# Two transformer blocks in one kernel: output parts that share a bank, copies tied to ScalarE, split remainders, gelu in stages, products ahead of the strips

## The chip, the core and the metric

The kernel runs on one core of a Trainium2 chip. The metric is device time in microseconds (us) of one execution. Five engines work beside each other, each through its own list of instructions in a fixed order: TensorE (PE, with PEld for its weight loads), VectorE (DVE), ScalarE (ACT), GpSimd (POOL) and SyncE (SP, which starts transfers). An engine stops at an instruction whose operands aren't ready, and everything behind it in its list stops too.

## The reference, cut to what matters

The input x has 512 tokens of 1024 float32 values and goes through two blocks.

```
block 1: p = rmsnorm(x) @ w_in            # q, k, v (8 heads of 64), u, vg (512 each), 8 forget gates
         att = softmax(q k^T/8 + cumsum(log sigmoid(forget)), causal) v
         u, vg = gelu(u), gelu(vg);  sg = u * (tril(w_spatial) @ rmsnorm(vg) + b)     # chunks of 128
         h = x + [att, sg] @ w_out;  h += conv_ffn(rmsnorm(h));  x = rmsnorm(h) * norm_final_g
block 2: mod = silu(c) @ w_ada + b        # six vectors: shift, scale, gate, twice
         p = modulate(rmsnorm(x)) @ w_in  # latents of q and kv, k_rope, cq, ck, cv
         o_ca  = chunk attention(rmsnorm(cq), rmsnorm(ck), cv, rel_bias)              # 8 heads of 64
         o_mla = latent attention: q, k from the latents, rmsnorm per head, rope      # 8 heads of 96
         x += g_a * ([o_mla, o_ca] @ w_out);  x += g_m * conv_ffn(modulate(rmsnorm(x)))
```

## The kernel before, in words

**Products.** Each float32 matrix product is three products of split operands: a weight is split into `whi` (a cast on ScalarE, L350) and a remainder `wlo` (raw minus `whi`, L351, on DVE, or on POOL where the plan says so), an activation into a pair of the same kind, and PE adds hi*hi, hi*lo and lo*hi in one of four PSUM banks with the tag `mm` (all through the helper at L372). `make_plan` (L279) lists the weight pieces in the order of use with a flag for POOL; pieces are loaded and split two ahead. Feature-major activations have one tile of 128 features by 512 tokens, x0 to x7.

**The order of PE.** It is the order in which the code issues. A `Fill` holds generators; `run(v)` lets them issue until about v ns of PE time are spent. `attention` (L619) walks over *strips*: a strip is one head's 128 queries against the 128, 256, 384 or 512 keys before their end. Block 1 has 32 strips, block 2 has 64: t0 to t31 of the chunk heads, t32 to t63 of the latent heads; t4, t8, t12 and so on are the narrow ones. A strip is: scores on PE (`s<-kh,qs` and `s<-kl,qs`), mask or bias and the row maximum on DVE (L597, a second small instruction reads the maximum out), exp on ScalarE (L601), transposes back on PE (`s<-ident,p`, L610), a copy `pt<-s` (L612), values on PE (`o<-vc,pt`). In PE's list the scores of strip t+2 stand before the transposes of strip t+1. Between these steps `fill.run` puts projections and output products whose inputs are there, and `bg.run` puts background jobs without PE work, or with little of it: norms, rope, and `final`, which scales x by block 1's last norm (x<-x,cols,mm, L942: two passes over x0 to x7, each pass from one bank).

**The order of the other engines.** A scheduler sorts their instructions by priority; background jobs get a lower one. The result is a fixed list per engine: where a list puts eight L942 instructions ahead of a strip's L597, that strip waits for them.

**The output product.** `gemm_part` (L403) multiplies one part of w_out with one pair of stacked attention tiles (`mix`), eight banks of 512 tokens each, and adds every bank to x on DVE (`x<-mm,x` L877 in block 1, `x<-mm,mod,x` L954 in block 2). It yields nothing until its own tiles are there. In block 2, `mix` tiles 0 to 3 come from the chunk heads in pairs, one tile every eight strips; part 0 needs the first two tiles, part 1 the other two. Parts 2 and 3 belong to the latent heads (`out_tail`).

**Norms of the latent heads.** `m_squares` (L1530) squares on POOL (`sqm<-mqk`, L1535), sums on DVE (`nw<-sqm`, L1536), a power on POOL (`nw<-nw,nhalf`, L526), a product on DVE (`mqk<-mqk,nw`, L1550), then the rope (`rt`, L1354 to L1357), and PE transposes (L1667). The chunk heads' norm does the same with `ca`, `sqc` and `ssc` (L1444 to L1457); PE transposes its result at L1633. The helper at L526 is the power of all norms.

**Gelu in block 1.** `gelu2` (L1108) takes one tile of 128x256: two steps on POOL, one on DVE (L1114), tanh on ScalarE, one on DVE (L1116), all issued at once. `qk(3)` evacuates a key projection at L1186 (`kf`), which PE waits for by way of its bank.

## Time and profile before

| | us |
|---|---|
| median of three runs (1226.94, 1228.15, 1228.16) | 1228.15 |
| the profiled execution | 1225.62 |
| its span | 1223.9 |
| PE busy | 1193.0 (97%) |
| DVE busy | 780.2 (64%) |
| ACT busy | 526.5 (43%) |
| POOL busy | 190.5 (16%) |

The profile is of one execution, 2.5 us under the median. From its start: projections of block 1 to about 70 us; attention 1 with its fill to about 215; the two feed-forward stages at 240 to 585 and at 866 to 1212; projections and norms of block 2 from 585; attention 2 from about 655 to 840; its output tail to 866. Busy time of PE is modelled: a matmul's row is longer than the distance to the next one (128x256: rows of 0.28 us that start every 0.115 us), so the idle time in rows of PE is what tells a wait. All times in what follows are us from the start of the span unless ns is said.

### The profile page before, as it was taken

The numbers are of one execution on the slowest core, as the hardware profiler recorded it, in microseconds if no ns is written. First come the engines' busy times: TensorE is split into PE (matmuls) and PEld (weight loads), VectorE is DVE, ScalarE is ACT, GpSimd is POOL, SyncE is SP. The second block draws the span as 40 slices with busy tenths as digits, with TensorE's granted clock in tenths as the row PEclk, the third lists the DMA queues.
The fourth block names the chain that finished last, engine by engine and source line by source line (L and its number), as shares of the span: only waits on it lengthen the run. The fifth ranks groups of instructions, "written<-read, shape, count | busy, mean of one in ns | idle before, by whom it ended". The sixth has DMA issues, their size and how long they took to land.

```text
span 1223.9 us, 17406 instructions
## 1 busy us (share of the span) xinstructions
PE 1193.0 (97%) x6730; PEld 1038.9 (85%) x6730; DVE 780.2 (64%) x1392; ACT 526.5 (43%) x946; POOL 190.5 (16%) x209
## 2 busy tenths in 40 slices
PE   9999898999999999999998989999999999999998
PEld 6898688988888888888998988899988888888887
DVE  6646777688888887433575878876675665653221
ACT  6535445454444443323434556655544444442110
POOL 2367301300000000000245472301200000000000
PEclk9999999999999999999999999999999999999999
DMA  7432222166666666433121333111133323233330
GB/s 237 120 102 78 82 82 61 53 188 196 200 192 190 193 190 190 144 98 128 58 86 57 87 109 104 36 36 36 53 123 102 103 86 104 93 89 112 114 110 18
DMA packets 42594, 135.78 MB, mean 111 GB/s; under 512 B 5120, under 2 KB 6016, under 8 KB 42512
## 3 DMA queue, kind: packets, MB, share of 16 engines
q1 hardware_dynamic: 34096, 106.84, 28.3%
q10 hardware_dynamic: 8208, 27.27, 7.4%
q8 instruction: 52, 0.85, 0.3%
q0 software_dynamic: 208, 0.57, 0.2%
q14 instruction: 30, 0.25, 0.1%
HBM read 128.37 MB, written 2.10 MB: 107 GB/s over the span
## 4 chain that ended last, share of the span: by engine, by line
PE 84%; DVE 6%; POOL 4%; issue 2%; ACT 2%; DMA 1%; SPq 0%; ACTq 0%; DVEq 0%; POOLq 0%
PE mm L372 74%; PE s L372 4%; PE o L372 3%; PE s L610 2%; POOL wlo L351 1%; ACT whi L350 1%; DVE wlo L351 1%; DVE s L597 1%; DVE ca L1457 1%; DMA x<-in_xT_dram 1%; POOL gelu L1111 0%; PE mm L1667 0%; DVE nt L557 0%; ACT p L601 0%; PE s L725 0%
## 5 line engine op out<-in xcount | busy, mean ns | idle before, releaser
L351 DVE TENSOR_TENSOR wlo<-wraw,whi 128x1024 fp32r<-128x1024 f32 (+4 forms) x182 | 210.3, 1157 | 180.6 <-ACT whi L350 179.5
L372 PE MATMUL mm<-xnh,whi 128*128 128x512 f32 (+1 forms) x832 | 310.8, 374 | 5.6 <-DVE x L877 2.7
L350 ACT CAST whi<-wraw 128x1024 fp32r<-128x1024 f32 (+4 forms) x194 | 191.6, 991 | 277.8 <-PE mm L372 260.2
L372 PE MATMUL mm<-xnl,whi 128*128 128x512 f32 (+1 forms) x832 | 309.7, 372 | 0.0
L372 PE MATMUL mm<-xnh,wlo 128*128 128x512 f32 (+1 forms) x832 | 309.7, 372 | 0.0
L372 PEld LDWEIGHTS mm<-xnh,whi 128*128 128x128 f32 x832 | 156.2, 188 | 33.5 <-DVE x L877 2.9
L372 PEld LDWEIGHTS mm<-xnh,wlo 128*128 128x128 f32 x832 | 156.1, 188 | 27.6
L372 PEld LDWEIGHTS mm<-xnl,whi 128*128 128x128 f32 x832 | 156.2, 188 | 26.7
L372 PE MATMUL mm<-gh,whi 128*128 128x512 f32 (+1 forms) x384 | 141.3, 368 | 1.1 <-DVE x L967 0.6
L372 PE MATMUL mm<-gh,wlo 128*128 128x512 f32 (+1 forms) x384 | 141.1, 367 | 0.0
L372 PE MATMUL mm<-gl,whi 128*128 128x512 f32 (+1 forms) x384 | 141.0, 367 | 0.0
L759 DVE SCALAR_TENSOR_TENSOR cv<-mm,cols,cv 128x510 f32<-128x510 f32 (+1 forms) x176 | 130.3, 745 | 2.5 <-ACT cv L757 0.5
L372 PE MATMUL mm<-whi,xnh 128*128 128x256 f32 (+3 forms) x304 | 96.5, 318 | 1.1 <-ACT xnh L842 1.1
L372 PE MATMUL mm<-wlo,xnh 128*128 128x256 f32 (+3 forms) x304 | 93.6, 308 | 0.2 <-DVE wlo L351 0.2
L372 PE MATMUL mm<-whi,xnl 128*128 128x256 f32 (+3 forms) x304 | 93.6, 308 | 0.1
L372 PEld LDWEIGHTS mm<-gh,whi 128*128 128x128 f32 x384 | 72.1, 188 | 13.5 <-DVE x L967 0.8
L372 PEld LDWEIGHTS mm<-gh,wlo 128*128 128x128 f32 x384 | 72.1, 188 | 12.1
L372 PEld LDWEIGHTS mm<-gl,whi 128*128 128x128 f32 x384 | 72.1, 188 | 12.0
L601 ACT ACTIVATE p<-s,st 128x128 f32<-128x128 f32 (+1 forms) x96 | 50.7, 528 | 70.4 <-DVE st L597 64.6
L1028 DVE CUSTOM_DVE_ANT_0 wada<-wada,cs,cols 128x1024 f32<-128x1024 f32 x48 | 61.5, 1282 | 28.9 <-DMA wada<-in_w_ada_dram 28.8
L372 PE MATMUL mm<-mix,whi 128*128 128x256 f32 (+1 forms) x288 | 73.8, 344 | 2.6 <-DVE x L877 1.5
L757 ACT ACTIVATE cv<-mm,cols 128x512 f32<-128x512 f32 x88 | 67.6, 773 | 0.0
(296 smaller groups left out, 1793.2 us busy)
## 6 DMA issues: line engine op xcount, KB each, us to landing
wraw<-in_w_up_dram SPq DMA_DIRECT2D x88, 512.0 KB, 3.6
wada<-in_w_ada_dram ACTq DMA_DIRECT2D x48, 512.0 KB, 3.7
wraw<-in_w_down_dram SPq DMA_DIRECT2D x32, 512.0 KB, 3.6
wraw<-in_w_out_dram SPq DMA_DIRECT2D x16, 512.0 KB, 3.7
wraw<-in_w_down_dram SPq DMA_DIRECT2D x16, 384.0 KB, 3.2
wraw<-in_w_qk_dram SPq DMA_DIRECT2D x8, 512.0 KB, 4.2
wraw<-in_w_v_dram SPq DMA_DIRECT2D x8, 256.0 KB, 4.9
x<-in_xT_dram SPq DMA_DIRECT2D x8, 256.0 KB, 6.5
```

The source lines that it names most:

```text
L350: nc.scalar.copy(hi[:, :n], raw[:, :n])
L351: (nc.gpsimd if pool else nc.vector).tensor_tensor(out=lo[:, :n], in0=raw[:, :n], in1=hi[:, :n].bitcast(F32), op=ALU.subtract)
L372: self.nc.tensor.matmul(out, lhsT, rhs, start=start, stop=stop, **kw)
L597: self.urgent = nc.vector.tensor_tensor_reduce(out=s[:, cs], in0=s[:, cs], in1=b, scale=1.0, scalar=3e38 if j == 0 else st[:, j - 1:j], op ...
L601: nc.scalar.activation(out=p[:, :nk], in_=s[:, :nk], func=AF.Exp, bias=st[:, len(parts) - 1:len(parts)], scale=-1.0, accum_out=hd["sums"](qi))
L610: self.nc.tensor.transpose(s[:, c], p[:, c], self.ident)
L757: nc.scalar.activation(out=t, in_=ps, func=AF.Identity, scale=w[2], bias=self.col(cb, n))
L759: nc.vector.scalar_tensor_tensor(out=t[:, d:], in0=ps[:, :512 - d], scalar=w[2 - d], in1=t[:, d:], op0=ALU.mult, op1=ALU.add)
L1028: nc.vector.tensor_tensor_reduce(out=w, in0=w, in1=self.cs, scale=1.0, scalar=self.col("b_ada_2", n), op0=ALU.mult, op1=ALU.add, accum_out ...
L1457: nc.vector.tensor_tensor(out=v3, in0=v3, op=ALU.mult, in1=ss[:, j, z, t].unsqueeze(2).to_broadcast([P, 4, 64]))
```

## The change

1. `gemm_first` replaces `gemm_part` for parts 0 and 1: both parts of an output tile add up in one bank (four matmul triples, then one addition to x). It yields nothing until the tiles of both parts are in `mix`. The plan lists these pieces in the order of use and flags parts 0 and 1 for POOL.
2. A remainder on POOL is made in steps of 256 columns.
3. Copies that `nc.any` spread over engines are ScalarE's: `pt`, `ca`, `kr`, `vc`, `mqk`, `vm`.
4. `gelu2` takes two tiles at once (128x512), yields between its stages, and its DVE steps have a late priority; the tiles have a pool of their own.
5. Block 1's fill has `turn(1)` right behind `spatial(1)`; block 2's fill has no `out1`; `final` moves from `cq0` to the second `mla`; the yield behind the rope tables is 3000, not 6000.
6. Ahead of attention 2, three rounds of `fill.run(1500)` and `bg.run(800)`; in it, the background rate is 1700 to strip 33, then 1200 (before: 1700 to strip 15, then 600).

```diff
         def parts(name, dest, skewed=()):
-            for p in range(4):
-                for g in range(2):
-                    plan.append((i[name][p, g], False, dest.get((p, g)), SKEW // 4 if p in skewed else 0))
+            for p, g in ((0, 0), (1, 0), (0, 1), (1, 1), (2, 0), (2, 1), (3, 0), (3, 1)):
+                plan.append((i[name][p, g], p < 2, dest.get((p, g)), SKEW // 4 if p in skewed else 0))
...
-            (nc.gpsimd if pool else nc.vector).tensor_tensor(
-                out=lo[:, :n], in0=raw[:, :n], in1=hi[:, :n].bitcast(F32), op=ALU.subtract)
+            step = 256 if pool else n
+            for o in range(0, n, step):
+                c = slice(o, min(o + step, n))
+                (nc.gpsimd if pool else nc.vector).tensor_tensor(
+                    out=lo[:, c], in0=raw[:, c], in1=hi[:, c].bitcast(F32), op=ALU.subtract)
...
+    def gemm_first(self, w, x, evac):
+        while not all(k in x for p in (0, 1) for k in PARTS[p]):
+            yield 0
+        cs = slice(0, 512)
+        for g in range(2):
+            hls = [self.weights([w[p, g]]) for p in (0, 1)]
+            for j in range(4):
+                ps = self.bank()
+                yield from self.part_tile(ps, [(hl[0], q, k) for p, hl in zip((0, 1), hls)
+                                               for q, k in enumerate(PARTS[p])], j, x, cs)
+                evac(4 * g + j, ps, cs)
...
-        self.nc.any.tensor_copy(out=pt[:, :nk], in_=s[:, :nk])
+        self.nc.scalar.copy(pt[:, :nk], s[:, :nk])
...
         def gelu2(v):
-            t = self.pp.tile([P, 512], F32, tag="p", name="gelu")[:, :256]
+            t = gl.tile([P, 2, 256], F32, tag="gl", name="gelu")
             nc.gpsimd.tensor_tensor(out=t, in0=v, in1=v, op=ALU.mult)
             nc.gpsimd.tensor_scalar(out=t, in0=t, scalar1=0.044715, scalar2=1.0, op0=ALU.mult,
                                     op1=ALU.add)
-            nc.vector.tensor_tensor(out=t, in0=t, in1=v, op=ALU.mult)
+            yield 800
+            with self.late():
+                nc.vector.tensor_tensor(out=t, in0=t, in1=v, op=ALU.mult)
...
             ("sp1", lambda: spatial(1)),
-            ("out0", lambda: self.gemm_part(i["w_out"], 0, mix, evac)),
             ("tu1", lambda: turn(1)),
-            ("out1", lambda: self.gemm_part(i["w_out"], 1, mix, evac)),
+            ("out0", lambda: self.gemm_first(i["w_out"], mix, evac)),
...
-            bg.add("final", final)
...
             if c == 0:
                 bg.add("kr", kr_rope())
+            else:
+                bg.add("final", final)
...
         def out0():
             bg.upto("final")
-            yield from self.gemm_part(i["w_out_2"], 0, mix, evac)
+            yield from self.gemm_first(i["w_out_2"], mix, evac)
...
-            ("out1", lambda: self.gemm_part(i["w_out_2"], 1, mix, evac)),
...
+        for _ in range(3):
+            fill.run(1500)
+            bg.run(800)
         self.attention(
             heads, fill,
             lambda t: 3000 if t < 0 else 2000 if t < 16 else 1600 if t < 34 else 500,
-            bg, lambda t: 1700 if t < 16 else 600, mix)
+            bg, lambda t: 1700 if t < 34 else 1200, mix)
```

What the change moves is seen in the engines' lists. First PE in block 2 at strips t21 to t23 before (`mm<-mix,w` are products of the output parts 0 and 1, `mm_7162` and so on their banks):

```order
L372 MATMUL mm_7150<-mix_6982,whi_7063 128x512 x2
L372 MATMUL mm_7150<-mix_6982,wlo_7064 128x512
L610 MATMUL s_7092<-ident_156,p_7097 128x128 x2
L372 MATMUL mm_7162<-mix_6587,whi_7063 128x512 x2
L372 MATMUL mm_7162<-mix_6587,wlo_7064 128x512
L372 MATMUL o_6985<-vc_5307,pt_7118 128x64
L372 MATMUL s_7167<-kh_6621,qs_6620 128x512
L372 MATMUL s_7167<-kl_6622,qs_6620 128x512
L372 MATMUL mm_7162<-mix_6982,whi_7063 128x512 x2
L372 MATMUL mm_7162<-mix_6982,wlo_7064 128x512
L610 MATMUL s_7133<-ident_156,p_7138 128x128 x3
L372 MATMUL mm_7191<-mix_6587,whi_7063 128x512 x2
```

In the list after, the same strips stand without them; `s_7116`, `s_7142` and `s_7162` are the scores of t21, t22 and t23 (and `s_7078` those of t20):

```order
L375 MATMUL s_7116<-kh_6650,qs_6649 128x256
L375 MATMUL s_7116<-kl_6651,qs_6649 128x256
L629 MATMUL s_7078<-ident_156,p_7083 128x128
L375 MATMUL o_7024<-vc_5271,pt_7111 128x64 x4
L375 MATMUL s_7142<-kh_6650,qs_6649 128x384
L375 MATMUL s_7142<-kl_6651,qs_6649 128x384
L629 MATMUL s_7116<-ident_156,p_7121 128x128 x2
L375 MATMUL o_7024<-vc_5271,pt_7136 128x64
L375 MATMUL s_7162<-kh_6650,qs_6649 128x512
L375 MATMUL s_7162<-kl_6651,qs_6649 128x512
L629 MATMUL s_7142<-ident_156,p_7147 128x128 x3
L375 MATMUL o_7024<-vc_5271,pt_7159 128x64 x2
```

From the scores of t20 to the transposes of t34 nothing but strips and some groups of four transposes of 128 columns stands in PE's list; the output products begin behind them.

DVE's list before, at strips t3 and t4 of block 2, has the first pass of `final` (`mm_6219` is its bank):

```order
L597 ISA s_6194,st_6197<-s_6194,bs_6026 128x512
L597 ISA st_6197 128x1
L942 SCALAR_TENSOR_TENSOR x0_83<-x0_83,cols_95,mm_6219 128x256
L687 TENSOR_TENSOR qs_6204<-mm_6210,qs_6204 64x512
L942 SCALAR_TENSOR_TENSOR x1_84<-x1_84,cols_95,mm_6219 128x256
L942 SCALAR_TENSOR_TENSOR x2_85<-x2_85,cols_95,mm_6219 128x256
L942 SCALAR_TENSOR_TENSOR x3_86<-x3_86,cols_95,mm_6219 128x256
L687 TENSOR_TENSOR qs_6207<-mm_6210,qs_6207 64x512
L351 TENSOR_TENSOR wlo_6254<-wraw_6251,whi_6253 128x256
L597 ISA s_6266,st_6269<-s_6266,bs_6108 128x128
```

After, that pass stands at t18 to t20 and the second at t21 and t22. DVE's list from t21 (`s_7116`) to t22 (`s_7142`) and the first of what follows:

```order
L616 ISA s_7116,st_7119<-s_7116,bs_6847 128x256
L616 ISA st_7119 128x1
L706 TENSOR_TENSOR qs_7039<-mm_7042,qs_7039 64x512
L716 SCALAR_TENSOR_TENSOR kl_7038<-mm_7085,gca_5258,kh_7037 64x512
L1666 TENSOR_SCALAR bs_7034<-bs_7034 128x512
L961 SCALAR_TENSOR_TENSOR x0_83<-x0_83,cols_95,mm_7054 128x256
L716 SCALAR_TENSOR_TENSOR kl_7041<-mm_7085,gca_5258,kh_7040 64x512
L616 ISA s_7142,st_7145<-s_7142,bs_6847 128x384
L616 ISA st_7145 128x1
L961 SCALAR_TENSOR_TENSOR x1_84<-x1_84,cols_95,mm_7054 128x256
```

Behind x7 of that pass come the sums, the scale and the products of the second latent group's norm, and only then the strip t23 (`s_7162`); the two small `st` rows between are the maxima:

```order
L961 SCALAR_TENSOR_TENSOR x7_90<-x7_90,cols_95,mm_7054 128x256
L1561 TENSOR_REDUCE nw_7067<-sqm_7098 128x4
L1561 TENSOR_REDUCE nw_7067<-sqm_7101 128x4
L1561 TENSOR_REDUCE nw_7067<-sqm_7104 128x4
L1568 TENSOR_SCALAR nw_7067<-nw_7067 128x16
L1575 TENSOR_TENSOR mqk_6856<-mqk_6856,nw_7067 128x768
L1575 TENSOR_TENSOR mqk_6857<-mqk_6857,nw_7067 128x768
L616 ISA s_7162,st_7165<-s_7162,bs_6847 128x512
L616 ISA st_7165 128x1
```

The second pass of `final` and the norm of `mqk_6856` and `mqk_6857` now both stand between the strips t22 and t23. The square sums in it come from POOL, whose list at that place has the output weights' remainders in steps, 16 instructions in four rows, ahead of the squares (`sqm`) and the power (`nw_7067`):

```order
L354 TENSOR_TENSOR wlo_6940<-wraw_6937,whi_6939 128x256 x4
L1667 MEMSET bs_6847 64x64
L354 TENSOR_TENSOR wlo_6990<-wraw_6987,whi_6989 128x256 x4
L354 TENSOR_TENSOR wlo_7439<-wraw_7436,whi_7438 128x256 x4
L354 TENSOR_TENSOR wlo_7448<-wraw_7445,whi_7447 128x256 x4
L1560 TENSOR_TENSOR sqm_7068<-mqk_6856 128x384
L1560 TENSOR_TENSOR sqm_7098<-mqk_6856 128x384
L1560 TENSOR_TENSOR sqm_7101<-mqk_6857 128x384
L1560 TENSOR_TENSOR sqm_7104<-mqk_6857 128x384
L1667 MEMSET bs_7034 64x64
L545 TENSOR_TENSOR nw_7067<-nw_7067,nhalf_161 128x16
```

In the list before, these remainders were on DVE (`wlo_7107`, `wlo_7147` and the like, one instruction of 1024 columns each).

## Rows read from the trace of the kernel before

**Rows 1.** The page, busy time of each engine and share of the span.

```profile
PE 1193.0 (97%) x6730; PEld 1038.9 (85%) x6730; DVE 780.2 (64%) x1392; ACT 526.5 (43%) x946; POOL 190.5 (16%) x209
```

**Rows 2.** Windows: length; engines' busy us (instructions); PE clock; DMA share; GB/s.

```profile
640.00:660.00 20.00, 16.59 (x135) 15.99 (x134) 13.56 (x17) 7.70 (x12) 15.04 (x9) 0.98 0.25 86
702.00:726.00 24.00, 20.00 (x168) 19.39 (x167) 17.57 (x45) 11.36 (x30) 17.14 (x23) 1.00 0.37 94
763.00:772.00 9.00, 8.29 (x61) 7.12 (x61) 8.09 (x23) 5.86 (x17) 3.58 (x6) 1.00 0.19 61
```

**Rows 3.** Waits of PE: total us, times, longest us.

```profile
PE mm L1633 <- DVE ca L1457: 3.4, 2, 2.2
PE mm L372 <- DVE kf L1186: 2.3, 1, 2.3
```

**Rows 4.** Timeline of DVE, block 1: start, us, instruction, idle before and releaser.

```profile
127.20 0.42 DVE L1114 TENSOR_TENSOR gelu<-gelu,uv 128x256 f32<-128x256 f32 x1 [1.22 <-POOL gelu L1112]
127.54 0.68 DVE L1186 TENSOR_TENSOR kf<-mm,rrow 128x512 f32<-128x512 f32 x1
```

**Rows 5.** Timeline of PE, block 1.

```profile
128.28 0.50 PE L372 MATMUL mm<-xnh,whi 128*128 128x512 f32 x1 [2.29 <-DVE kf L1186]
...
148.86 0.70 PE L372 MATMUL mm<-uv,wsp 128*128 128x256 f32 x2 [2.59 <-DVE mix L745]
```

**Rows 6.** Timeline of POOL at the start of attention 2.

```profile
652.95 2.67 POOL L351 TENSOR_TENSOR wlo<-wraw,whi 128x1024 fp32r<-128x1024 f32 x1
655.77 2.34 POOL L351 TENSOR_TENSOR wlo<-wraw,whi 128x1024 fp32r<-128x1024 f32 x1 [0.16 <-ACT whi L350]
```

**Rows 7.** Timeline of DVE, block 2, from there to strip t16.

```profile
652.91 5.81 DVE L1457 TENSOR_TENSOR ca<-ca,ssc 128x256 f32<-128x256 f32 x4 [3.01 <-POOL ssc L526]
...
682.20 2.83 DVE L942 SCALAR_TENSOR_TENSOR x<-x,cols,mm 128x256 f32<-128x256 f32 x7
...
702.59 0.70 DVE L597 CUSTOM_DVE_ANT_0 s<-s,bs 128x512 f32<-128x512 f32 x1 [1.17 <-PE s L372]
...
703.81 2.01 DVE L1457 TENSOR_TENSOR ca<-ca,ssc 128x256 f32<-128x256 f32 x4
...
712.16 0.76 DVE L697 SCALAR_TENSOR_TENSOR kl<-mm,gca,kh 64x512 fp32r<-64x512 f32 x1
...
717.08 0.96 DVE L1550 TENSOR_TENSOR mqk<-mqk,nw 128x768 f32<-128x768 f32 x1 [3.02 <-POOL nw L526]
...
725.64 0.28 DVE L597 CUSTOM_DVE_ANT_0 s<-s,bs 128x128 f32<-128x128 f32 x1
```

**Rows 8.** Windows of 3 us at the start of attention 2, as rows 2.

```profile
658.00:661.00 3.00, 2.55 (x14) 2.36 (x15) 2.17 (x5) 1.10 (x2) 0.11 (x1) 0.72 0.17 49
661.00:664.00 3.00, 3.00 (x21) 3.00 (x21) 2.12 (x3) 2.13 (x4) 0.00 (x0) 0.71 0.29 64
```

**Rows 9.** Chain of waits, block 2: start, us, engine and line.

```profile
665.26 2.07 PE mm L372 x18
...
679.40 0.44 PE s L610 x4
...
684.13 0.84 PE o L372 x8
```

**Rows 10.** Groups by line and shape: xcount, busy us, mean ns, idle before.

```profile
L942 DVE SCALAR_TENSOR_TENSOR x<-x,cols,mm 128x256 f32<-128x256 f32 x16 | 6.8, 473 | 0.2
...
L351 POOL TENSOR_TENSOR wlo<-wraw,whi 128x1024 fp32r<-128x1024 f32 x12 | 29.3, 2443 | 6.8 <-ACT whi L350 6.7
...
L601 ACT ACTIVATE p<-s,st 128x512 f32<-128x512 f32 x24 | 16.5, 688 | 14.2 <-DVE st L597 11.6 <-PE mm L372 2.4
...
L1535 POOL TENSOR_TENSOR sqm<-mqk 128x384 f32<-128x384 f32 x8 | 7.5, 932 | 12.8 <-ACT p L601 5.3 <-PE s L610 3.8 <-DVE nw L1536 3.5
...
L687 DVE TENSOR_TENSOR qs<-mm,qs 64x512 fp32r<-64x512 f32 x8 | 5.5, 688 | 1.1 <-ACT qs L686 0.9
...
L1536 DVE TENSOR_REDUCE nw<-sqm 128x4 f32<-128x384 f32 x8 | 4.4, 545 | 0.1
```

## What the rows say of the change: the prediction

> **What bounds the kernel now.** I read the page's busy times first: PE is busy 97% of the span, DVE 64%, ACT 43%, POOL 16% [rows 1]. The number of PE's instructions stays as it was, so the change can only win from the time in which PE waits, or add to it. Next come the windows of both attention stages. Of the 20 us before strip t0 of block 2, PE is busy 16.6; of the 24 us around strips t11 to t16, it is busy 20.0, while POOL works 17.1 and DVE 17.6; in 763 to 772, where PE's list already holds bare strips before, it is still busy 8.3 of 9 [rows 2]. The list of PE's waits then names who ends them: `kf` at L1186 and `ca` at L1457, both by DVE [rows 3]. The timelines show what stood ahead of them: `kf` is behind a gelu step that itself waited 1.22 us for POOL [rows 4], and PE's product waits 2.29 us for that [rows 5]; at 652.91, four `ca` instructions take 5.81 us [rows 7].
>
> **Step A, block 1.** The gelu steps go late in DVE's list, behind `kf`: of the 2.29 us, all goes; the wait of 2.59 us for `mix` (L745) at 148.86 [rows 5] stays, since `turn(1)` stands right behind `spatial(1)` and has no output product between. The additions to x become 8 instead of 16; at one or two of them PE waits for the bank, and I put 0.7 us on that. The copies that go to ScalarE and the four remainder tiles per block that go from DVE to POOL lie beside PE's work: cost nothing, gain nothing, unless POOL is late for a weight. Four tiles at 2.44 us on POOL [rows 10] are 9.8 us, and one late tile holds PE for at most those 2.4 us. A = -3, between -6 (the spatial wait goes too) and +1.
>
> **Step B, ahead of strip t0 of block 2.** PE waits 3.4 us in all for `ca` [rows 3], and behind the wait the granted clock is 0.72 and 0.71 of full for two windows of 3 us [rows 8]: 6 x 0.285 = 1.7 us more. The change puts 42 products of 256 columns there. 18 such take 2.07 us [rows 9], 0.115 each, so 42 take 4.8 us: longer than the wait. These 4.8 us are not new, they are taken from later strips. B = -4.8, between -5.5 and -2 (the next wait in the chain, for `qs`, then shows).
>
> Why the four `ca` took 5.81 us is seen beside them: POOL ran two remainders of 1024 columns from 652.95 to 658.1 [rows 6], and the same four instructions at 703.81 took 2.01 us [rows 7]. The Trainium skill has a rule for it ("SBUF — State Buffer", section "Who interferes with whom"): a VectorE instruction with two SBUF inputs and a GpSimd one that reads SBUF keep each other out for the whole instruction. The trace agrees, 5.81 against 2.01 us. By this rule steps of a quarter hold such an instruction for 0.6 us at a time, not 2.4: at most 4 x 0.6 on top of 2.01, 4.4 us instead of 5.81. B would stay what it is, since the products cover either.
>
> **Step C, strips t8 to t18.** From the DVE instruction of strip t11 (702.59) to that of t16 (725.64) are 23.05 us [rows 7], in a window where PE is idle 4.0 us [rows 2]: DVE and a power on POOL (3.02 us of waiting on it) set the pace. After, DVE has in these strips no copies of `pt`, `vm` or `mqk` and fewer remainders, and the PE time with it is unchanged. C = -4, between -5.5 (everything idle in t8 to t18) and -1 (ScalarE, which has the copies, is then late for the exp: 0.69 us each [rows 10]).
>
> **Step D, strips t18 to t34.** Here the change takes work from PE and gives work to DVE. Part 0 of the output product began at t21 before; `gemm_first` waits for all four tiles of the chunk heads, the last of which is ready after t31. In PE's list from t18's scores to t23's transposes are then 12 products of 256 columns (1.4 us), six pairs of scores (17 times 256 columns, 2.0 us), 25 transposes (0.11 each by the row of four in 0.44 us [rows 9]: 2.8 us), 26 value products at 0.105 [rows 9] (2.7 us) and four products with `ms`, taken as eight of 0.11 (0.9 us): 10 us. In DVE's list between the same points stand, by rows of the same forms:
> - both passes of `final`, 16 at 2.83/7 = 0.40 us [rows 7]: 6.5
> - five strips' mask and maximum, 0.28 to 0.70 [rows 7]: 2.7
> - one `mix` and two `qs` at 0.69 [rows 10], two `kl` at 0.76 [rows 7], one `bs`: 4.0
> - four sums at 0.55 [rows 10] and a scale: 2.4
> - the wait for the power, 3.02, and two `mqk` at 0.96 [rows 7]: 4.9
>
> That is 20.5 us, and the exp of t23 on ScalarE (0.69 [rows 10]) with its sum read out adds 0.9. Rows of DVE overlap by some 0.07 us (0.47 is the mean row of L942 [rows 10], 0.40 its share in the run of seven), so I take 1.2 off for the 17 others: 20 us against 10. PE runs out of what it can do at the transposes of t22 and t23 and waits 10 us. Two things come on top. POOL's list has four remainder tiles (9.8 us) and four squares (0.93 each [rows 10]) ahead of that power, and the last tile is cast on ScalarE in t18; DVE's first sum stands ahead of the last two x of the first pass, so I take 3 us of waiting for it. Behind t23 come ten more strips without fill; in 763 to 772 four to five such strips lose 0.7 us [rows 2], so ten lose 1.5 to 2. D = 10 + 3 + 2 = +15. Ends: +7, where POOL is in time, scores run ahead of DVE at t18 and the bare strips pass as fast as before; +20, where the POOL wait doubles and ScalarE, which has four copies of `vm`, a cast of 1024 columns and the first `qs` between the exps of t18 and t19, adds its own.
>
> PE's clock is weighed here too. After the wait at 658 it was 0.72 and 0.71 [rows 8], and in D PE waits longer. The Trainium skill's page "TensorE: Matmul & The Clock Gate" (section "HAM oscillation — how this bites in real kernels") says that idle gaps send the array back to half its clock, and that each gap pays anew. The rows agree for one gap: 1.7 us. By the rule D would be 16 to 18, but PE has idle time to lose in that stretch, so in the sum it has nothing.
>
> **The sum.** -3 - 4.8 - 4 + 15 = +3.2 us. The profiled execution took 1225.62 us, so one after would take 1228.8. The median of the runs is 1228.15, 2.53 us above it: forecast 1231.4. The bound of what can be told from no change is 0.2%, 2.45 us, so it is slower beyond 1230.6.
>
> **Rivals.**
> 1. *The gap in the fill is shorter than its list, and the kernel gets faster.* The mechanism is slack: the scores of two strips stand ahead of each transpose, DVE idles in t14 to t18, where PE has fill, and each strip's exp needs only its own strip. If D costs +6, the sum is -3 - 4.8 - 4 + 6 = -5.8, or 1222.3. It decides at D under 9.3 us. For it: the bare strips at 763 to 772 lost little with 8.1 of 9 us of DVE busy [rows 2]. Against it: DVE's list is fixed, both passes of `final` and the norm stand ahead of t23, and none of those 20 us of work can be passed by.
> 2. *Gains and loss cancel.* With D between 9.4 and 14.2 the sum lies within 2.4 us either way; also if A, B and C give half (-6) and D is its 7 (+1). Time 1228.
> 3. *POOL becomes the bound.* The steps of remainders and DVE's two-input instructions hold each other, so that squares, power and a weight come late together. The four `ca` lost 3.8 us to two tiles [rows 6, 7]; block 2 has four tiles more on POOL, 7.6 us at that rate. Then D = 20 and C = 0: -3 - 4.8 + 20 = +12, or 1240. For it: POOL was busy 17.1 of 24 us at t11 to t16 already [rows 2]. Against it: a step holds for a quarter of the time.
>
> **How the numbers follow.** The forecast's case (D from 14.3 to 19, 1230.6 to 1236) has 0.34, the faster one 0.31, the cancelling one 0.21, POOL as the bound 0.14. Slower: 0.34 + 0.14 = 0.48; the same: 0.21; faster: 0.31. The range runs from 1220 (A, B and C as taken, D = 4) to 1241 (the third rival); the forecast's own is 1230 to 1236. What is left out on either side is about one in ten.
>
> **What would show it.** In the profile after, strips t19 to t24 of block 2 take over 15 us, PE waits 2 to 5 us at t22's transposes and 5 to 9 at those of t23, both ended by ScalarE's exp and behind it by DVE; POOL's squares start right behind the remainders, and the strip's L597 of t23 starts right behind the two `mqk`. `kf` no longer ends a wait, no wait for `ca` over 1 us stands ahead of t0, and the clock holds 1.00 there. The forecast is wrong if PE's waits in t18 to t34 come to under 9 us, or if a new wait, for a weight's remainder or for the exp, shows over 3 us elsewhere.

## The result, and the profile after

The changed kernel takes 1243.86 us (median of runs from 1239.95 to 1249.09) beside 1227.55 for the kernel before on the same chip: 1.0139 times as long, interval 1.009 to 1.0187. That is slower, as forecast, but by 16.3 us, where the forecast's sum had +3.2, and the median lies above the range's end of 1241 (two of the four executions, 1239.95 and 1240.48, lie just under it). The profiled execution took 1247.23 us (span 1245.0), 21.6 more than that of before.

The page after, busy times; it answers to [rows 1]:

```profile
PE 1205.5 (97%) x6730; PEld 1050.2 (84%) x6730; DVE 747.0 (60%) x1312; ACT 535.3 (43%) x974; POOL 216.3 (17%) x257
```

DVE has 33 us less and POOL 26 more; PE has the same 6730 instructions and 12.5 us more of them. So PE was not only made to wait: of the 21.1 us by which the span grew, 8.6 are waiting (39.5 us without work against 30.9), and 12.5 are PE running slower.

Windows show both. A row's loss is its length less PE's busy time, plus busy time times (1 - granted clock). The first fence holds windows of the kernel before that [rows 2] don't have (block 1; strips t1 to t10 and t17 to t29 of block 2; the stretch where the last norm begins), with the columns as there:

```profile
80.00:240.00 160.00, 147.12 (x923) 128.75 (x922) 109.72 (x262) 73.15 (x167) 52.40 (x58) 1.00 0.26 76
660.00:702.00 42.00, 41.50 (x329) 40.85 (x328) 30.33 (x73) 22.02 (x53) 13.94 (x14) 0.97 0.28 76
726.00:763.00 37.00, 36.94 (x254) 33.77 (x253) 31.31 (x68) 25.60 (x61) 13.26 (x14) 1.00 0.38 114
763.00:790.00 27.00, 26.03 (x187) 23.29 (x188) 22.62 (x60) 16.78 (x47) 12.13 (x15) 1.00 0.13 40
845.00:890.00 45.00, 44.10 (x340) 42.28 (x339) 30.31 (x56) 26.40 (x50) 10.68 (x14) 1.00 0.16 50
```

The same windows, and the two of [rows 2], after:

```profile
80.00:240.00 160.00, 150.90 (x921) 132.34 (x920) 96.67 (x229) 74.00 (x165) 64.90 (x74) 0.97 0.26 76
640.00:660.00 20.00, 20.00 (x171) 20.00 (x170) 10.13 (x13) 7.87 (x15) 16.38 (x15) 1.00 0.25 81
660.00:702.00 42.00, 39.62 (x311) 38.98 (x310) 23.41 (x54) 25.45 (x65) 18.40 (x25) 0.96 0.29 79
702.00:726.00 24.00, 22.56 (x177) 21.66 (x176) 17.44 (x44) 12.06 (x34) 17.23 (x22) 1.00 0.40 115
726.00:763.00 37.00, 22.16 (x136) 20.45 (x135) 22.59 (x59) 17.13 (x46) 26.19 (x38) 0.67 0.28 87
763.00:790.00 27.00, 26.48 (x185) 23.70 (x185) 15.95 (x46) 17.65 (x50) 6.72 (x7) 0.95 0.00 1
845.00:890.00 45.00, 42.20 (x326) 40.89 (x325) 29.87 (x60) 19.34 (x40) 10.17 (x13) 0.96 0.21 71
```

| Stretch | loss before | loss after | difference | forecast |
|---|---|---|---|---|
| 80 to 240 (A) | 12.9 idle + 0 clock | 9.1 + 4.5 | +0.7 | -3 |
| 640 to 702 (B) | 3.9 + 1.6 | 2.4 + 1.6 | -1.5 | -4.8 |
| 702 to 726 (C) | 4.0 | 1.4 | -2.6 | -4 |
| 726 to 790 (D) | 1.0 | 15.4 + 7.4 | +22 | +15 |
| 845 to 890 | 0.9 | 2.8 + 1.7 | +3.6 | none |

The clock of a window is a mean that counts its idle time too, so D's 7.4 is summed from windows of 4 us. The differences add up to +22, where the two profiled executions differ by 21.6. The clock column has two digits, so a row can be off by half a us, and the agreement is no closer than that.

The waits of PE after (total, times, longest); `ca` and `kf` of [rows 3] have no row any more:

```profile
PE s L629 <- ACT p L620: 18.1, 9, 7.4
PE mm L375 <- ACT sq L515: 2.5, 1, 2.5
...
PE s L375 <- DMA kh<-kh: 1.4, 1, 1.4
...
PE mm L375 <- DVE mix L764: 1.1, 1, 1.1
PE s L375 <- DMA kl<-kl: 1.0, 1, 1.0
```

Three waits for an exponential make up 14.84 us of D. PE's timeline there (the scores of t18, then x4, x2 and x4, the transposes of t19, t21 and t23):

```profile
729.65 0.42 PE L375 MATMUL s<-kh,qs 128*128 128x384 f32 x1
...
738.25 0.89 PE L629 MATMUL s<-ident,p 128*128 128x128 f32 x4 [2.48 <-ACT p L620]
...
750.78 0.69 PE L629 MATMUL s<-ident,p 128*128 128x128 f32 x2 [7.36 <-ACT p L620]
...
759.74 1.11 PE L629 MATMUL s<-ident,p 128*128 128x128 f32 x4 [5.00 <-ACT p L620]
```

The chain of waits through that stretch (start, us, engine and line) has nothing of PE from 735.79 to 759.74:

```profile
735.81 4.84 POOL wlo L354 x7
740.65 0.79 POOL sqm L1560
...
746.92 2.74 DVE x L961 x7
749.66 1.39 DVE nw L1561 x3
...
751.33 2.91 POOL nw L545
754.27 0.97 DVE mqk L1575
...
755.30 1.10 POOL rt L1381
...
758.41 0.47 POOL mqk L1386
758.90 0.34 ACT p L620
...
759.74 1.11 PE s L629 x4
```

In words: remainders of weights on POOL, then the squares of the second latent group, `final`'s second pass, the sums, the power, the products, the rope. These are two pieces of background (the norm of the second `mqk`, `final`) and the remainders, all within 23 us. And the exponentials wait for more than their masks. The next three fences show POOL's remainders there, the masks of t18, t21 and t23 on DVE, and the exponentials of t21 and t23 on ScalarE:

```profile
729.51 2.83 POOL L354 TENSOR_TENSOR wlo<-wraw,whi 128x256 fp32r<-128x256 f32 x4
...
732.38 8.28 POOL L354 TENSOR_TENSOR wlo<-wraw,whi 128x256 fp32r<-128x256 f32 x12
```

```profile
730.49 0.56 DVE L616 CUSTOM_DVE_ANT_0 s<-s,bs 128x384 f32<-128x384 f32 x1
...
742.72 0.43 DVE L616 CUSTOM_DVE_ANT_0 s<-s,bs 128x256 f32<-128x256 f32 x1
...
756.01 0.69 DVE L616 CUSTOM_DVE_ANT_0 s<-s,bs 128x512 f32<-128x512 f32 x1
```

```profile
750.16 0.47 ACT L620 ACTIVATE p<-s,st 128x256 f32<-128x256 f32 x1 [4.74 <-DVE nw L1561]
...
758.90 0.69 ACT L620 ACTIVATE p<-s,st 128x512 f32<-128x512 f32 x1 [4.88 <-POOL mqk L1386]
```

t18's and t23's masks bound the stretch that D reckoned with; t21's is done at 743.2, its exponential starts 7 us later and waits for `nw`, a sum of squares: its tile comes from the pool `pp2`, three tiles shared with the squares (`sqm`) and the rope's products.

### The profile page after: what moved, and what is told of

Read it like the earlier page. It is cut to its first block, busy times and chain, and to the rows that moved or that the text cites. A ratio compares the mean times of both kernels' runs of the same rounds, so it can differ in the third digit from the quotient of the medians.

```text
span 1245.0 us, 17431 instructions
## 1 busy us (share of the span) xinstructions
PE 1205.5 (97%) x6730; PEld 1050.2 (84%) x6730; DVE 747.0 (60%) x1312; ACT 535.3 (43%) x974; POOL 216.3 (17%) x257
## 4 chain that ended last, share of the span: by engine, by line
PE 87%; DVE 4%; POOL 4%; ACT 2%; issue 2%; DMA 1%; SPq 0%; ACTq 0%; DVEq 0%; POOLq 0%
PE mm L375 77%; PE s L375 4%; PE o L375 3%; PE s L629 2%; POOL wlo L354 1%; DVE s L616 1%; DMA x<-in_xT_dram 1%; DVE nt L576 1%; PE mm L1693 0%; DMA cs<-in_c_dram 0%; POOL nw L545 0%; ACT p L620 0%; PE s L744 0%; ACT whi L349 0%; PE r L375 0%
## 5 line engine op out<-in xcount | busy, mean ns | idle before, releaser
L354 DVE TENSOR_TENSOR wlo<-wraw,whi 128x1024 fp32r<-128x1024 f32 (+5 forms) x174 | 200.5, 1155 | 182.9 <-ACT whi L349 181.9
L1047 DVE CUSTOM_DVE_ANT_0 wada<-wada,cs,cols 128x1024 f32<-128x1024 f32 x48 | 61.5, 1282 | 30.8 <-DMA wada<-in_w_ada_dram 30.8
L545 POOL TENSOR_TENSOR rstd<-rstd,nhalf 128x2 f32<-128x2 f32 x6 | 5.1, 858 | 363.9 <-DVE rstd L554 363.9
```

What stands on the lines that cost most here:

```text
L354: (nc.gpsimd if pool else nc.vector).tensor_tensor(out=lo[:, c], in0=raw[:, c], in1=hi[:, c].bitcast(F32), op=ALU.subtract)
L545: self.nc.gpsimd.tensor_tensor(out=x, in0=x, in1=e, op=ALU.pow)
L1047: nc.vector.tensor_tensor_reduce(out=w, in0=w, in1=self.cs, scale=1.0, scalar=self.col("b_ada_2", n), op0=ALU.mult, op1=ALU.add, accum_out ...
```

## Experiments

Each time stands beside that of the kernel before on the same chip (1227.6 to 1228.1 us). The last columns are read from each profile: PE's longest wait for an exponential in the whole kernel (in e8, e13 and e18 it lies in block 1), and PE's busy time and clock in the 37 us from 726. PE's waits for other things are not in the column: e1 has one of 5.9 us for `mix`, e2 one of 5.6 for a bank that `final` reads, e4 one of 6.6 for `att`, e14 and e15 one of 3.7 and 3.4 ahead of a score.

| Run | Edit to the changed kernel | us | ratio to before, interval | wait | busy, clock |
|---|---|---|---|---|---|
| after | - | 1243.86 | 1.0139, 1.009 to 1.0187 | 7.4 | 22.2, .67 |
| e1 | `final` early | 1239.73 | 1.0097, 1.0082 to 1.0112 | 5.6 | 24.7, .71 |
| e2 | parts apart | 1237.71 | 1.0081, 1.0054 to 1.0108 | 4.7 | 24.1, .82 |
| e3 | remainders on DVE | 1239.61 | 1.0101, 1.0084 to 1.0118 | 6.1 | 23.0, .68 |
| e6 | e3 + e1 | 1236.33 | 1.0068, 1.0053 to 1.0083 | 7.9 | 24.7, .72 |
| e7 | e6 + e2 | 1226.21 | 0.9995, 0.9979 to 1.0012 | 5.2 | 30.8, .91 |
| e4 | squares' own tiles | 1249.44 | 1.0173, 1.0158 to 1.0188 | 5.2 | 26.2, .77 |
| e10 | four tiles | 1240.96 | 1.011, 1.0082 to 1.0137 | 6.0 | 22.9, .63 |
| e12 | e7 + e10 | 1225.91 | 0.9986, 0.9972 to 0.9999 | 4.0 | 30.8, .95 |
| e5 | scores repeated | 1243.07 | 1.0124, 1.0107 to 1.0141 | 3.6 | 28.6, .77 |
| e11 | rate of before | 1228.86 | 1.0006, 0.999 to 1.0022 | 6.2 | 29.2, .86 |
| e14 | e11 + e1 | 1229.23 | 1.0016, 1.0002 to 1.003 | 1.7 | 30.2, .86 |
| e15 | e14 + e10 | 1230.56 | 1.0016, 1.0001 to 1.0031 | 2.0 | 29.5, .91 |
| e16 | before + new rate | 1235.76 | 1.0063, 1.0045 to 1.0081 | 1.3 | 31.9, 1.00 |
| e8 | e7 + rate, rope, copies | 1220.58 | 0.9938, 0.9918 to 0.9957 | 0.9 | 34.5, 1.00 |
| e13 | e8 + e10 | 1215.28 | 0.9897, 0.9868 to 0.9926 | 0.9 | 35.2, 1.00 |
| e17 | e13, joined, POOL | 1226.59 | 0.9996, 0.9978 to 1.0014 | 5.2 | 29.4, .86 |
| e18 | e13, joined | 1219.17 | 0.9923, 0.9907 to 0.994 | 0.9 | 32.8, 1.00 |
| e19 | e13, POOL | 1219.64 | 0.9932, 0.9914 to 0.9949 | 1.0 | 34.8, 1.00 |

**One part undone at a time (e1, e2, e3), and together (e6, e7).**

```diff
 e1:  bg.add("rope", rope())
+     bg.add("final", final)          # and no longer behind the second mla
 e2: -yield from self.gemm_first(i["w_out_2"], mix, evac)
     +yield from self.gemm_part(i["w_out_2"], 0, mix, evac)
     +("out1", lambda: self.gemm_part(i["w_out_2"], 1, mix, evac)),   # and the plan's order
 e3: -plan.append((i[name][p, g], p < 2, ...
     +plan.append((i[name][p, g], p < 2 and name == "w_out", ...
```

> The kernel after, with the job `final` back in `cq0` (its 16 instructions on DVE then stand at strips t0 to t3). Theory 1 (DVE's list: both passes of `final` ahead of the masks of t18 to t23 make the wait): PE's waits for the exp in t18 to t24 fall from 14.8 us (2.5 + 7.4 + 5.0) to 5 to 8, the clock recovers sooner, time 1231 to 1236. Rival (POOL's chain: the remainders ahead of the squares, and the exp behind both): the waits stay over 11 us, time 1240 or more.

> The kernel after, with parts 0 and 1 of block 2's output product one after the other again (part 0 may start with the first two tiles, plan in that order; their remainders stay on POOL in quarters). Theory 1 (the gap in the fill is the root, DVE's and POOL's lateness only shows because of it): waits for the exp in t18 to t34 under 4 us, clock 1.00 there, time 1221 to 1227. Rival (DVE and POOL are late by themselves): waits over 8 us stay, time over 1234.

> The kernel after, with block 2's four remainder tiles of parts 0 and 1 back on DVE, whole (four instructions, 4 x 1.23 = 4.9 us more on DVE, 11.1 us of steps less on POOL). Theory 4 (the two runs before have shown that neither the place of `final` nor the gap in the fill is enough: POOL is late, its remainders stand ahead of the squares, and tiles, banks and exps wait behind them): PE's waits in t18 to t24 fall from 14.8 us to 5 to 9, time 1231 to 1237. Rival, theory 1 (DVE's list is what is too long): DVE has more to do, the waits stay over 13 us, time 1242 or more.

> The kernel after with two edits: block 2's remainders on DVE, whole, and `final` in `cq0`. Theory 4 with theory 1 as its second half: POOL's lateness and the 6.5 us of `final` each cover the other, and with both gone the waits in t18 to t34 fall under 5 us, time 1226 to 1232. Rival, theory 5 (a stretch of 15 strips without fill costs by itself, since each strip's chain is longer than PE's part of it): over 8 us of waits stay, time 1236 or more.

> The kernel after with three edits: remainders of block 2 on DVE, `final` in `cq0`, and parts 0 and 1 of block 2 apart. What is left of the change is block 1's part, the copies on ScalarE, the background rates and the products ahead. Theory 4 with 1 and 5: no wait over 2 us in t8 to t34, time 1219 to 1225, faster than before. Rival (ScalarE's copies or the background rates hold the strips by themselves): a wait over 3 us stays in t8 to t34, time 1228 or more.

Each alone gives back 0.4 to 0.6% of the time before, which the intervals hardly tell from after's wide one, and leaves long waits. With the parts apart (e2) PE still waits 8.2 us for exponentials in block 2 and 5.6 us for a bank behind `final`, so closing the gap in the fill does not free the strips by itself. All three together give 1.44%, about what the single ones add up to (0.42, 0.58, 0.38), and end where the kernel before stands. Of the expectations, e2 and e6 came out as their rivals; e1, e3 and e7 fell between the two times stated.

**The exponentials' tiles (e4, e10, e12).**

```diff
 e4:  sq = nq.tile([P, 384], ...)     # a pool of its own, two tiles
 e10: -self.pp = self.pool("pp2", 3, ctx=ctx)
      +self.pp = self.pool("pp2", 4, ctx=ctx)
```

> The kernel after, with the squares of the latent heads' norms in two tiles of their own, not in the three that the exps write to. Theory 2 (the exp of t21 waits 4.7 us not for its mask but for a tile that a square holds until DVE sums it): the wait of 7.4 us falls to under 3, time 1232 to 1237. Rival (DVE's list alone): the wait stays within 1.5 us of 7.4 or moves to the next strip, time 1240 or more.

> The kernel after with one number changed: the pool that the exps of block 2 share with the squares and the rope's tiles has four tiles, not three. Theory 2 (the exps of t21 and t23 had their masks 6.8 and 1.9 us before they started; each waited for a tile that a square or a rope product held): the waits of 7.4 and 5.0 us fall to 3 to 7 in all, time 1232 to 1238. Rival (the masks themselves are late by DVE's list, and a fourth tile is taken by the next square): the waits stay over 10 us, time 1241 or more.

> The kernel with three edits (remainders of block 2 on DVE, `final` in `cq0`, parts apart), and four tiles in that pool. Theory 2: its wait of 5.2 us before the exp of t22, whose mask was done 8.4 us before the exp, goes to under 1.5; time 1219 to 1224. Rival (the wait moves to another tile or list): 1225 or more.

The shared tiles end the wait of 7.4 us in the trace, yet a fourth tile gives no gain that the intervals can tell (1.011 beside 1.0139; 0.9986 beside 0.9995), and tiles of their own for the squares, which also reorder the lists, are no faster (1.0173). All three came out as their rivals (e10 by its waits; its time is just under the 1241 stated). The trace of e10 shows why: the wait for a tile moves one strip on. t22's mask is done at 740.6, its exponential starts at 745.73 behind a sum of squares, and PE waits 6.00 us for it; then t24's mask comes only at 755.42, behind the norm on DVE, and PE waits 5.18 us.

**The clock (e5).** The scores of t20, t22 and t24 are computed 8, 9 and 14 times.

```diff
-        for j, (q, k) in enumerate(qk):
+        for j, (q, k) in list(enumerate(qk)) * rep:
```

> The kernel after, with the scores of strips t20, t22 and t24 of block 2 made 8, 9 and 14 times over into the same bank (7.5 us more work for PE, in the time in which it waits). Theory 3 (the clock at half through 738 to 766 costs 6 to 8 us, because the chain there is partly PE's own): the clock stays at 0.9 or more in that stretch and the time falls by 3 to 7 us, to 1237 to 1241. Rival (PE's half clock lies in time that it waits anyway): no change or up to 4 us slower, 1243 to 1248, whatever the clock does.

The repeated scores brought the clock from .67 to .77 and PE's busy time from 22.2 to 28.6, and the time stayed as it was, as the rival had it. So products laid into the waits cost nothing; whether a full clock would gain there stays open, since .77 is not 1.00.

**The background's rate (e11, e14, e15, e16).**

```diff
 e11: -bg, lambda t: 1700 if t < 34 else 1200, mix)
      +bg, lambda t: 1700 if t < 16 else 600, mix)
 e16: the other way round, in the kernel before
```

> The kernel after with block 2's background rate as before (1700 to strip 15, then 600; not 1700 to strip 33, then 1200). Theory 6 (the higher rate issues the norms of the second latent group and `final` close together in t18 to t24, where POOL's power, squares and rope come in one chain): jobs are spread over more strips, PE's waits fall from 14.8 to 6 to 10, time 1231 to 1237. Rival (remainders ahead of the squares decide, at any rate): waits over 12 us, time 1241 or more.

> The changed kernel with the background's rate of before (1700 to strip t15, then 600) and `final` back ahead of the first output parts; joined parts, remainders on GpSimd, ScalarE's copies and the products ahead stay. Theory (the rate and `final`'s place are the whole cause of block 2's loss): the wait of 6.2 us at strip t19 that e11 kept goes, none of the waits for an exponential is over 5 us, 1219 to 1224 us. Rival (joined parts or the remainders on GpSimd cost by themselves): 1227 us or more, with waits of over 5 us left between 726 and 772 us.

> e14 with four tiles instead of three for the exponentials, squares and rope products. Theory (shared tiles make an exponential wait only where a norm's products stand ahead of it in the lists, which is as much spread out here): 2 to 5 us under e14, 1215 to 1221 us. Rival (they are a cause only together with the packed norms): within 1.5 us of e14.

> The kernel before with the changed kernel's rate of the background (1700 to strip t33, then 1200) and nothing else of the change. Theory (the rate costs by itself, since it packs the second latent group's norms into strips t18 to t24): 5 to 12 us slower than before, 1233 to 1240 us, with waits of 4 us or more for exponentials between 726 and 772 us. Rival (it costs only beside `final` behind the second chain or the joined parts): at most 2 us slower than before.

The old rate alone takes 15 us back, the most of any single edit and more than its theory had (1231 to 1237). What is left is one wait of 6.2 us behind `final`, whose rows now stand together. DVE of e11:

```profile
734.76 5.18 DVE L961 SCALAR_TENSOR_TENSOR x<-x,cols,mm 128x256 f32<-128x256 f32 x13
...
740.32 0.29 DVE L616 CUSTOM_DVE_ANT_0 s<-s,bs 128x128 f32<-128x128 f32 x1
```

In e14 `final` is early again and the longest wait for an exponential is 1.7 us, as the theory said; the time is not (1229.2, not 1219 to 1224), and a fourth tile does not change it (e15, as its rival had it). The rate and `final` are therefore not the whole cause. More than half of PE's idle time from 726 to 763 in e14 is one wait ahead of the scores of t20. POOL, DVE and PE of e14:

```profile
725.43 2.82 POOL L354 TENSOR_TENSOR wlo<-wraw,whi 128x256 fp32r<-128x256 f32 x4
...
728.30 2.78 POOL L354 TENSOR_TENSOR wlo<-wraw,whi 128x256 fp32r<-128x256 f32 x4
```

```profile
731.90 0.55 DVE L1562 TENSOR_REDUCE nw<-sqm 128x4 f32<-128x384 f32 x1 [4.87 <-POOL sqm L1561]
```

```profile
733.76 0.35 PE L375 MATMUL s<-kh,qs 128*128 128x256 f32 x1 [3.65 <-issue]
```

DVE's sum waits 4.87 us for a square that stands behind two rows of remainders on POOL; behind the sum come t19's mask and the `mix` product, which ends at 733.67. The profile names no releaser for PE's wait, but in e1 the same wait (5.9 us) is put down to `mix`. So with the rate and `final` undone, POOL's remainders still hold up the strips; e15 has the same pattern, with 3.44 us.

In the kernel before, the new rate alone costs 7.8 us. The time is in the theory's range; the waits of 4 us or more for exponentials are not there (the longest is 1.3). One wait of 5.76 us for `att` shows where most of it goes: behind the norm's power, products and rope, which now stand ahead of it. Ahead of them stands a load of the bias `bs`, which lands at 751.14; POOL's list has its use of `bs` in front of the power. PE and chain of e16:

```profile
763.70 1.09 PE L725 MATMUL s<-ident,att 128*128 128x128 f32 x4 [5.76 <-DVE att L717]
```

```profile
751.87 2.87 POOL nw L526
...
755.89 1.02 POOL rt L1354
756.92 1.40 POOL rt L1355
...
762.29 0.66 DVE x L954
762.96 0.61 DVE att L717
```

**A better version (e8, e13).** e8 adds to e7 the old rate, the rope's yield of 6000 and block 2's copies (all but `pt`) on any engine; e13 a fourth tile.

```diff
-            yield 3000
+            yield 6000
-            nc.scalar.copy(ca_slice(t, 0, 0), ps[:, 32:288])     # and kr, vc, mqk, vm
+            nc.any.tensor_copy(out=ca_slice(t, 0, 0), in_=ps[:, 32:288])
```

> As the one with three edits, and block 2's background rates, the yield behind the rope tables and its copies of `ca`, `kr`, `vc`, `mqk`, `vm` as before too (the `pt` copies stay on ScalarE, the products ahead of t0 stay). If the rates or these copies cost, it is faster than the one with three edits by over 2 us; if they win, slower by as much. By the sum of the prediction, block 1 (-3) and the products ahead (-4.8) are left: time 1219 to 1224. Rival (block 1 and the products ahead gain nothing on the chip): 1226 to 1230.

> The kernel that is fastest so far (three edits, rates and block 2's copies as before; 1220.6) with four tiles in that pool. Its waits for the exp are 3.5 us in six pieces. Theory 2: one to three of these go, 1217 to 1220. Rival (with the jobs spread, no exp waits for a tile any more): no change, 1219 to 1222.

e13 is the fastest by its median, 1.0% under the kernel before; the intervals do not tell it from e8. e8 came out as expected, e13 below its range. It keeps the products ahead of t0, block 1's part of the change, and `pt` on ScalarE.

**Joined parts and remainders on POOL (e17, e18, e19)**, each laid on e13 with the diffs of e2 and e3 reversed.

> e15 with block 2's copies of ca, kr, vc, mqk and vm left to the scheduler's choice again and the rope's yield at 6000, joined parts kept. Theory (rate, `final`, shared tiles and the copies fixed to ScalarE are the losses; the joined parts are none): 1213 to 1218 us, as e13 or better. Rival (the joined parts cost 3 us or more): 1218 us or more.

> e13 with the first two output parts of block 2 joined (their remainders on VectorE). Theory, now that e17's wait of 5.2 us stands behind 8.26 us of remainders in one row on GpSimd (12 of 256 columns) and e16 has no such wait before its output parts: the remainders on GpSimd are the cost and the joined parts are not: 1215 to 1219 us. Rival (the stretch without fill that the joined parts leave costs, as the forecast had it): 1222 us or more, with the engine's idle time between 726 and 763 us more than 5 us.

> e13 with the remainders of block 2's first two output parts on GpSimd in quarters (the parts stay apart). Theory (the remainders are the cost): 1221 to 1227 us, with a wait for an exponential behind a row of remainders on GpSimd. Rival (the joined parts are): 1215 to 1219 us.

With neither the time is 1215.3, with the joined parts 1219.2, with the remainders on POOL 1219.6, with both 1226.6. The single steps are not told apart from e13 by their intervals, but both together are from either one. The single steps add up to 8.3 us and both cost 11.3; that they cost more together than their sum is not shown, since the intervals are as wide as that difference. e17 came out as its rival; e19 fell between its two expectations, and e18 at the edge of the theory's. The rows suggest how the two work together. The profiled execution of e17 is its slowest (1232.78), so its waits are above the usual. POOL's row of twelve quarters in e17, and what PE then waited:

```profile
732.69 8.28 POOL L354 TENSOR_TENSOR wlo<-wraw,whi 128x256 fp32r<-128x256 f32 x12
```

```profile
744.76 0.90 PE L629 MATMUL s<-ident,p 128*128 128x128 f32 x3 [5.22 <-ACT p L620]
```

The same row in e19:

```profile
728.33 8.35 POOL L355 TENSOR_TENSOR wlo<-wraw,whi 128x256 fp32r<-128x256 f32 x12
```

There PE is busy 34.8 of 37 us and its longest wait for an exponential is 1.0: output products stand between the strips, and the late squares behind POOL's row meet no strip that has nothing else before it. In both runs the row also holds an instruction on DVE with one input, the change of sign of the bias. DVE of e19:

```profile
732.21 4.75 DVE L1667 TENSOR_SCALAR bs<-bs 128x512 f32<-128x512 f32 x1
```

In e17 it took 3.97 us; the median of its six in either run is 0.42. In e19 it ends 0.3 us after POOL's row.

## Why the forecast came out as it did

The sign was right, and so was the place of the largest loss; the size was not. By the steps:

- **A, forecast -3, measured +0.7.** The idle time fell by 3.8 us: `kf` ends no wait, the `mix` wait of [rows 5] is 1.07 instead of 2.59, and the waits for additions to x went from 4.2 to 1.8 us, where the forecast had put 0.7 on them. The clock took it back: 0.97 over 150.9 us of work is 4.5 us, where before it was 1.00. The step that failed is "in the sum it has nothing", said of the clock. The copies on ScalarE, put at nothing, did not cost nothing either: PE's waits in block 1 for `pt` went from 0.4 to 2.4 us. The clock is 0.66 in the window from 116 to 121 and 0.57 from 216 to 220; such waits (1.01 us to 117.11, 1.24 to 214.08) stand at or ahead of their start. From 188 to 192 it is 0.62, behind a wait of 1.80 for an addition to x.
- **B, forecast -4.8, measured -1.5.** The window before t0 is full, as forecast (20.00 of 20, clock 1.00), and no wait for `ca` is left. But once PE came sooner to strip t0, its scores waited 1.4 and 1.0 us for the DMAs of `kh` and `kl`: the forecast named `qs` as the next wait, not these. The end of -2 was missed.
- **C, forecast -4, measured -2.6**, inside its ends.
- **D, forecast +15, measured +22.** This is above the upper end of +20, with half clock counted. The waits sum to 14.84 us against 13 in the forecast (10 and 3); they stand at t19, t21 and t23, not at t22 and t23. PE's list of 10 us was right: from t18's scores to t23's transposes 30.1 us pass, less the waits 15.2, of which 9 were run at half clock: 10.7 at full. The chain beside it was taken too short: DVE's list with t23's exponential was taken as 20 us and the wait for POOL as 3, so 23 in all, where the 30.1 us passed. From t18's mask to t23's DVE took 25.5 us (730.49 to 756.01). In them it waits 3.02 us for the power and 3.29 for the first square, as forecast, and 2.12 for `qs`, which ScalarE casts behind a late weight; the forecast kept that for its upper end. The exponential came 2.2 us after its mask for want of a tile, which the forecast did not have. POOL's four remainders took 11.1 us (2.83 + 8.28), not 9.8, and the squares came right behind them, as said.
- **What came on top** is the clock. Granted clock in D, windows of 4 us:

```profile
738.00:742.00 4.00, 3.75 (x19) 3.75 (x20) 0.69 (x4) 2.55 (x8) 3.43 (x5) 0.57 0.67 215
...
746.00:750.00 4.00, 0.00 (x0) 0.00 (x0) 3.95 (x11) 0.00 (x0) 0.00 (x0) 0.50 0.42 93
...
762.00:766.00 4.00, 4.00 (x20) 3.89 (x20) 2.84 (x10) 1.21 (x4) 0.94 (x3) 0.52 0.00 0
766.00:770.00 4.00, 3.83 (x31) 3.32 (x30) 2.43 (x7) 3.42 (x9) 3.64 (x2) 1.00 0.01 2
```

  Behind the first wait PE runs at 1.2 GHz (0.50) until 766. The seven windows from 738 to 766 put that at 7.4 us (1.6, 0.7, 0, 1.6, 0.4, 1.1 and 1.9). Of it, what stands ahead of the waits at 750.78 and 759.74 only shortened those waits; the 6.3 us of work from 759.74 to 766 are on the chain, so the clock's own price there is about 3 us, an estimate, and e5 does not contradict it. The Trainium skill's page "TensorE: Matmul & The Clock Gate", section "HAM oscillation — how this bites in real kernels", says of its case, a wait in every round of a loop, that each gap pays anew. The windows of D agree, and so do the three half-clock stretches of A after; in block 1 before, waits of 2.29 and 2.59 us [rows 5] left the clock at 1.00, so not every gap paid. The forecast set the rule aside.
- **The tail, +3.6, was no term.** At 877.14 PE waits 2.52 us for `sq`. That wait is in every run with `final` late and the new rate (after, e2, e3, e4, e5, e10) and in none of the others.

Two steps of the reasoning failed most. The first is the clock, "in the sum it has nothing", on the ground that PE has idle time to lose in D. That holds for the part of D's half clock that lies ahead of another engine's wait, but not for some 3 us at its end, nor for A and the tail, where 4.5 and 1.7 us were lost; in all PE's work took 12.5 us more. The second is the length of D's chain, 23 us in the forecast and 30.1 in the trace, with A's and B's gains smaller on top.

D's account of the chain, a stretch without fill in PE's list beside a long list on DVE and POOL, is what the trace shows. The stretch alone is not dear: the joined parts in e18 leave PE busy 32.8 of 37 us at full clock and win against before. What made it dear is what stood beside it. D counted these lists as they stand; it did not ask what packed them. That was the new rate, with `final`'s new place: undoing the rate alone gives 15 us (e11), and it costs 7.8 us with nothing else of the change (e16). The rate was quoted in the change and had no term in the sum. But it is not the only way back: with the new rate kept, undoing `final`, the joined parts and the remainders on POOL gives 17.6 us (e7). Rival 3, POOL as the bound, was the nearest in size (1240) and has POOL's row in the chain. Remainders on DVE alone gave only 4 us (e3), while in e17 they make 7 us of difference to e18: POOL is one of three stages of one chain.

Still open: the shares of the rope's yield and of the copies within e8, and the rest of what holds e14 and e15 at 1229 to 1231 (PE is idle 6.8 and 7.5 of 37 us there, at clocks of .86 and .91, and one wait is about half of it). No run undoes block 1's part, the `pt` copies or the products ahead of t0, so what is said of A and B rests on the trace of the changed kernel alone.

## What to carry to other kernels

A background rate is a placement: when a change raises it, list which pieces land in the same strips, and add up their DVE and POOL rows in the order of the fixed lists, not the fill alone. A stretch without fill, and a long row on a side engine, cost some 4 us each here, within the noise, and 11 together, so try such a pair as a square of four kernels. When PE's waits are added up, price the clock behind each of them too, and only where PE's work is on the chain.

## What the runs showed of the hardware

- A remainder of 1024 columns takes POOL 2.44 us in one piece [rows 10] and 0.69 to 0.71 per quarter, 2.8 us in four: four tiles cost 1.3 us more in quarters.
- PE was at half clock from 738 to 766 although it worked through 4.00 of 4 us at the end of that stretch; it returned to 1.00 in the window from 766.
- A clock of 0.97 over 160 us took back a gain of 3.8 us of waiting in block 1, with no wait over 1.8 us there to announce it; before, waits of 2.29 and 2.59 us in the same block left the clock at 1.00.
- Quarters on POOL let two-input products on DVE in, but not the one-input `bs`. Four `ca` took 3.09 us beside eight quarters in the changed kernel, against 5.81 beside two whole tiles [rows 6, 7]; one `bs` took 4.75 us beside twelve quarters in e19 and 3.97 in e17, against 0.42 at the median.
